# Memory keys and values, and the recurrence's values, in 512-column products instead of 256

## Chip, cores and metric

The kernel runs on one core of a Trainium2 chip. The metric is the device time of one execution in microseconds (us), the median of several runs. A smaller number is better. The profile is a trace of one execution on the same kind of chip.

## The reference, cut to what matters

Two layers of a decoder trunk on 512 tokens of width 1024, with 256 memory tokens, all in float32:

```python
mem_n = rmsnorm(mem, mem_norm)
for l in range(DEPTH):                                   # DEPTH = 2
    h = rmsnorm(x, norm_mix)
    (..., g_q, g_f, g_i, g_g, m_q, gate_logits) = split_cols(h @ w_in)
    y_a = a_b * causal_conv3(a_c * a_x, conv_w)          # branch A
    y_b = dsa_attention(q, k, d_v, iq, ik, iw)           # branch B: top-128 of the keys
    hv = g_i.reshape(b, s, HG_HEADS, HG_DV)              # the recurrence's values
    o_c = hgrn2_chunkwise(hq, hk, hv, log_f)             # branch C
    mk, mv = jnp.split(mem_n @ mem_w_kv, 2, axis=-1)     # 512 columns of keys, 512 of values
    mk = rmsnorm(mk.reshape(b, MEM_TOKENS, MEM_HEADS, MEM_HEAD_DIM), mem_k_norm)
    ...                                                  # branch M: cross-attention to mk, mv
    merged = sum(gates[n] * (branches[n] @ w_lift[n]) for n in range(4))
    x = x + merged @ w_out
    x = x + ffn(rmsnorm(x, norm_ffn))
```

## The kernel before, in words

Every large product runs as three matmuls. A float32 operand is split into a high part in the matmul's reduced format and a low rest, and `mm3` (lines 269 to 272) adds high by high, high by low and low by high into one accumulator tile. One matmul has a stationary tile of 128x128 and a moving operand of 256 or 512 columns.

Weights come through `Chunk` (line 211). One transfer on the SP queue brings 1024 KB (for instance 1024 rows by 256 columns, or 512 rows by 512 columns) into `w_raw`, which has 2 buffers. Two conversions follow, each for half of the chunk: ScalarE (ACT) writes `w_hi` and VectorE (DVE) writes `w_lo` (line 225). These pairs have 3 buffers (`W_BUFS`), and they are written with `high_priority`.

The accumulators are tiles of 128x512 float32 in three groups: `mm` with 3 buffers, `at` with 2, `tr` with 3. Products use `mm`. Attention scores, the index scores and the recurrence use `at`. Transposes and small sums use `tr`.

The order of the instructions on each engine is not the order in the source. The kernel is built with `schedule_with_timeline_sim=True`: a planner walks a simulated time line and gives each engine the ready instruction of the lowest number, where a number is the place in the source, lowered by 3000 in `high_priority`. An accumulator buffer goes to the first planned instruction that asks for it. The result is a fixed list for each engine.

The stages that the change touches:

1. **Start.** `mem_in_T` transposes the normalised memory into `mt`. `mem_kv(l)` (line 427) then makes keys and values of layer l, first for layer 0, woven with `first_h` (which makes `h` from `x`), and after `rope_tables` for layer 1. It goes over four column blocks of 256, two of keys and two of values. For each block it takes one chunk (all 1024 rows) and for each of the two token tiles 24 matmuls of 256 columns (`tokens`, line 250). For keys it copies the result to `ku`, sums squares per head, computes one norm for two heads by two token tiles, scales, transposes, and writes `kv` as a high and a low part. A transfer of 512 KB per block stores them in `kv_dram`.
2. **Mixer, the part around the attention of branch B.** In each layer `lift(3, y_m)` runs woven with `sel`, the selection of the 128 largest index scores (lines 824 and 825 on DVE). Then `weave(chain(lift(0, y_a), values(hv)), attend(0..3), R2)` writes one step of the first chain and three steps of attention in turn. `lift(n)` has four steps of 48 matmuls for two gate tiles and 24 for two tiles of `y`, all of 512 columns. `values(hv)` (line 667) has two steps, each with one chunk of 256 columns and four token tiles of 24 matmuls of 256 columns. `attend(t)` has two steps of four heads: scores into `at` (lines 685 and 686), a biased minimum on DVE (line 698), exponentials and scaling on ACT into `prob`, transposes (line 709) copied to `pt`, and products with `vt` (line 715) that end in `y_b`.
3. **Recurrence** (`hgrn`). `logits` makes `zf`, `zq`, `zg` (line 880 takes them out of `mm`). Its pool reuses the memory of the attention's tiles. `head` uses `hv`.

Of the kernel before, what the change touches and what calls it, by code (L numbers as in the profile page):

```python
# [12 lines left out]
F32 = mybir.dt.float32  # L13
# [56 lines left out]
def hybrid_trunk(ctx: ExitStack, tc: tile.TileContext, x, mem, positions, norm_mix, w_in, conv_w,  # L70
# [19 lines left out]
    def A(dst, src, func, **kw):  # L90
        name = tables.get(func)
        if name is not None and name != table["set"]:
            load = act.preload_act_table_set(name)
            for u in table["users"]:
                tc.add_manual_dep(load.ins, u.name, order, reason="table set")
            table.update(set=name, load=load.ins, users=[])
        i = act.activation(dst, src, func, **kw)  # L97
        if name is not None:
            tc.add_manual_dep(i.ins, table["load"].name, order, reason="table set")
            table["users"].append(i.ins)  # L100
        return i

    def mm_ps():
        return pmm.tile([P, 512], F32, name="mm")
# [4 lines left out]
    def tr_ps():  # L109
        return pat.tile([P, 512], F32, name="tr", bufs=TR_BUFS)  # L110

    def f(ap):
        return ap.bitcast(F32)
# [62 lines left out]
    def col(i):  # L176
        return prm[:, i:i + 1]
# [21 lines left out]
    def rstd_into(dst, ms, scratch, n):  # L199
        rstd(dst, ms, scratch(n), scratch(n))  # L200

    def small(n, name="small", bufs=12):
        return consts.tile([P, 8], F32, name=name, bufs=bufs)[:, :n]
# [32 lines left out]
    def wchunk(src, kt, n):  # L236
        return Chunk(src, kt, n)

    def pair(a, k, s=slice(None)):
        return a[0][:, k, s], a[1][:, k, s]  # L240
# [11 lines left out]
    def tokens(w, a, t, ps, k0=0, kt=None):  # L252
        kt = w.kt if kt is None else kt
        for k in range(k0, k0 + w.kt):
            mm3(ps, pair(a, k, slice(t * P, (t + 1) * P)), w.at(k - k0), k == 0, k == kt - 1)
# [11 lines left out]
    def mm3(ps, a, b, first, last):  # L267
        ah, al = a
        bh, bl = b
        pe.matmul(ps, ah, bh, start=first, stop=False)  # L270
        pe.matmul(ps, ah, bl, start=False, stop=False)  # L271
        pe.matmul(ps, al, bh, start=False, stop=last)  # L272
# [104 lines left out]
    mem_r = small(2, name="mem_r", bufs=1)  # L377
    mem_sq = sp.tile([P, D], F32, name="mem_sq")
    mt = (sp.tile([P, KD, MEM], F32R, name="mt_hi"), sp.tile([P, KD, MEM], F32R, name="mt_lo"))
    mem_r2, mem_r4 = small(4, name="mem_r2", bufs=1), small(4, name="mem_r4", bufs=1)  # L380

    def mem_in_T():
        for c in range(KD):
            ps = tr_ps()
            for t in range(2):
                pe.transpose(ps[:, t * P:(t + 1) * P], mem_in[:, t, c * P:(c + 1) * P], ident)
            A(mt[0][:, c, :], ps[:, :MEM], AF.Copy, scale=g_mem(c))
            dve.scalar_tensor_tensor(mt[1][:, c, :], ps[:, :MEM], g_mem(c), f(mt[0][:, c, :]),
                                     op0=OP.mult, op1=OP.subtract)
        for t in range(2):  # L390
            A(mem_sq, mem_in[:, t, :], AF.Square, scale=D ** -0.5, accum_out=mem_ss[:, t:t + 1])
        rstd_into(mem_r, mem_ss, small, 2)
        dve.tensor_copy(mem_r4.rearrange("p (a b) -> p a b", b=2), mem_r[:, :, None].to_broadcast([P, 2, 2]))
        dve.tensor_mul(mem_r2, mem_r4, mem_r4)

    norms = []
# [29 lines left out]

    def mem_kv(l):
        kv = sp.tile([P, 4, 2, 2, MEM], F32R, name="kv", bufs=1)
        for q in range(2):
            w = wchunk(mem_w_kv[l][:, q * 256:(q + 1) * 256], KD, 256)  # L430
            kus = []
            ms, r = small(4), small(4, "mk_r", 2)
            for t in range(2):
                ps = mm_ps()[:, :256]
                tokens(w, mt, t, ps)
                ku = sp.tile([P, 2, P], F32, name="ku", bufs=3)
                with tc.high_priority(offset=AHEAD):
                    A(ku.rearrange("p a b -> p (a b)"), ps, AF.Copy)
                for j in range(2):
                    sq = sp.tile([P, P], F32, name="mk_sq", bufs=2)  # L440
                    A(sq, ku[:, j, :], AF.Square, scale=P ** -0.5, accum_out=ms[:, 2 * t + j:2 * t + j + 1])
                kus.append(ku)
            dve.tensor_mul(ms, ms, mem_r2)
            rstd_into(r, ms, small, 4)
            dve.tensor_mul(r, r, mem_r4)
            for t in range(2):
                for j in range(2):
                    dve.tensor_scalar(kus[t][:, j, :], kus[t][:, j, :], r[:, 2 * t + j:2 * t + j + 1], None, op0=OP.mult)
            for j in range(2):
                ps = tr_ps()[:, :MEM]  # L450
                for t in range(2):
                    pe.transpose(ps[:, t * P:(t + 1) * P], kus[t][:, j, :], ident)
                hi, lo = kv[:, 2 * q + j, 0, 0, :], kv[:, 2 * q + j, 0, 1, :]
                A(hi, ps, AF.Copy, scale=col(76 + l))
                dve.scalar_tensor_tensor(lo, ps, col(76 + l), f(hi), op0=OP.mult, op1=OP.subtract)
            nc.scalar.dma_start(kv_dram[l][:, 2 * q:2 * q + 2, 0], f(kv[:, 2 * q:2 * q + 2, 0]))
            yield
        for q in range(2):
            w = wchunk(mem_w_kv[l][:, 512 + q * 256:512 + (q + 1) * 256], KD, 256)
            for t in range(2):  # L460
                ps = mm_ps()[:, :256]
                tokens(w, mt, t, ps)
                ps = ps.rearrange("p (h d) -> p h d", d=P)
                hi, lo = (kv[:, 2 * q:2 * q + 2, 1, e, t * P:(t + 1) * P] for e in range(2))
                A(hi, ps, AF.Copy, scale=mem_r[:, t:t + 1])
                dve.scalar_tensor_tensor(lo, ps, mem_r[:, t:t + 1], f(hi), op0=OP.mult, op1=OP.subtract)
            nc.scalar.dma_start(kv_dram[l][:, 2 * q:2 * q + 2, 1], f(kv[:, 2 * q:2 * q + 2, 1]))
            yield
    mem_in_T()
    steps(mem_kv(0), first_h())  # L470
    rope_tables()
# [29 lines left out]
    def mixer(l, h, norms, cm, cf):  # L501
# [11 lines left out]
        def lift(n, y, merged, last=None):  # L513
            def gates(m):
                gw = wchunk(w_in[l][:, C_GATE + n * D + m * P:C_GATE + n * D + (m + 2) * P], KD, 256)
                gs = [gate_tile()[:, :S] for _ in range(2)]
                for g, ps in zip(gs, features(gw, h, (0, 1))):
                    with tc.high_priority(offset=AHEAD):
                        dve.tensor_mul(g, ps, r_b)
                    sigmoid(g, g, mix.tile([P, S], F32, name="gate_e", bufs=1))  # L520
                return gs

            look = LOOK[l][n] == "1"
            ahead = gates(0) if look else None
            for m in range(0, KD, 2):
                if look:
                    gs, ahead = ahead, gates(m + 2) if m + 2 < KD else None
                else:
                    gs = gates(m)
                lw = wchunk(w_lift[l, n][:, m * P:(m + 2) * P], 4, 256)  # L530
                pls = features(lw, y, (0, 1))
                for i in range(2):
                    g, pl = gs[i], pls[i]
                    with tc.high_priority(offset=AHEAD):
                        if n == 3:
                            dve.tensor_mul(merged[:, m + i, :], g, pl)
                        else:
                            dve.tensor_mul(g, g, pl)
                            dve.tensor_add(merged[:, m + i, :], merged[:, m + i, :], g)
                    if last is not None:  # L540
                        last(m + i)
                yield
# [19 lines left out]
        def weave(main, back, ratio):  # L562
            for _ in main:
                for _ in range(ratio):
                    next(back, None)
            for _ in back:
                pass
# [97 lines left out]
                        yield  # L665

        def values(hv):
            for q in range(2):
                w = wchunk(w_in[l][:, C_GI + q * 256:C_GI + (q + 1) * 256], KD, 256)
                for t in range(NT):  # L670
                    ps = mm_ps()[:, :256]
                    tokens(w, h, t, ps)
                    A(hv[:, t, q * 256:(q + 1) * 256], ps, AF.Copy, scale=r_t[:, t:t + 1])
                yield

        with pool_("dsa") as dp:
            qS = dp.tile([P, 8, S], F32R, name="qS")
# [170 lines left out]
            hvs = cm.enter_context(ExitStack())  # L848
            hv = hvs.enter_context(pool_("hv", "left")).tile([P, NT, 512], F32, name="hv")
            with pool_("att", "left") as dp2:  # L850
                weave(chain(lift(0, y_a, merged), values(hv)), chain(*(attend(t, dp2, y_b) for t in range(NT))), R2)

        with pool_("hgrn") as hp:
            y_c = new_y()
# [261 lines left out]
```

## Time and profile before

| | |
|---|---|
| median of 3 runs | 2047.9 us (2047.63 to 2047.9) |
| profiled execution, its time | 2047.48 us |
| profiled execution, its span | 2045.4 us |
| PE (TensorE matmul) busy | 2034.5 us |
| DVE busy, ACT busy | 1269.3 us, 1017.5 us |
| matmuls | 10348 |

A row of a time line or of the chain reads: start in us, duration in us, engine, source line, operation, output tile <- input tiles, shape, count; in brackets the idle time just before it and what ended it. "PEld" is the load of a stationary tile, which overlaps "PE". The ends of matmuls are modelled, so that a matmul shown with 0.39 us can have its successor 0.23 us after its start. The distance between starts is therefore the pace of PE, and its busy time is not. Rows of a "windows" view give, for a stretch of the span, the busy time and the count of each engine, the granted TensorE clock ("PEclk") and the share of the transfer engines in use.

### The profile page before, as it was taken

Reading aid. Unit: us, or ns where it says so; the run is one execution under the profiler, and the core shown is the slowest. Engines: PE = TensorE matmul, PEld = TensorE weight load, DVE = VectorE, ACT = ScalarE, POOL = GpSimd, SP = SyncE. Lnnn points to the kernel's source line nnn. Section 1 sums busy time; section 2 is a strip of 40 time slices with the busy share of each in tenths; the row PEclk is TensorE's granted clock in tenths of the full one; section 3 lists DMA queues with packets and bytes.
Section 4 is the critical chain, followed back from the end, with each engine's and each line's share of the span. In section 5 each row is a group of like instructions: output and inputs, shape, how many; then the busy total and the mean of one; then the engine's idle time right before and its main releaser. Section 6 shows DMA issues by size and latency. Waiting matters only on the chain.

```text
span 2045.4 us, 26581 instructions
## 1 busy us (share of the span) xinstructions
PE 2034.5 (99%) x10348; PEld 1715.8 (84%) x10348; DVE 1269.3 (62%) x2507; ACT 1017.5 (50%) x1834; POOL 9.8 (0%) x33
## 2 busy tenths in 40 slices
PE   8999999999999999999999999999999999999999
PEld 8998988888888888888889898888888888888887
DVE  6779998547676544334457889963777754533442
ACT  7653655766665423223355456576767633322331
POOL 0000000000000000000000000000000000000000
PEclk9999999999999999999999999999999999999999
DMA  7632232223233232233243213322223322323322
GB/s 253 220 89 94 68 93 93 64 71 93 78 118 113 83 103 93 93 105 102 87 155 94 88 58 107 97 76 63 83 83 101 126 90 96 103 75 111 97 79 93
DMA packets 187709, 203.79 MB, mean 100 GB/s; under 512 B 4270, under 2 KB 176384, under 8 KB 187456
## 3 DMA queue, kind: packets, MB, share of 16 engines
q1 hardware_dynamic: 183872, 193.56, 29.8%
q10 hardware_dynamic: 3552, 8.41, 1.1%
q8 instruction: 81, 1.33, 0.3%
q14 instruction: 44, 0.36, 0.1%
q0 software_dynamic: 160, 0.13, 0.0%
HBM read 191.60 MB, written 10.49 MB: 99 GB/s over the span
## 4 chain that ended last, share of the span: by engine, by line
PE 99%; DMA 1%; DVE 0%; ACT 0%; SPq 0%; issue 0%; DVEq 0%
PE mm L270 30%; PE mm L272 30%; PE mm L271 30%; PE tr L715 1%; PE tr L709 1%; PE at L686 1%; PE at L685 1%; PE at L272 1%; PE at L270 1%; PE at L271 1%; DMA w_raw<-in_mem_w_kv_dram 1%; PE at L963 0%; PE at L937 0%; PE tr L653 0%; PE tr L754 0%; PE tr L972 0%
## 5 line engine op out<-in xcount | busy, mean ns | idle before, releaser
L270 PE MATMUL mm<-h_hi,w_hi 128*128 128x512 f32 x1664 | 653.0, 393 | 0.0
L271 PE MATMUL mm<-h_lo,w_hi 128*128 128x512 f32 x1664 | 652.1, 392 | 0.0
L272 PE MATMUL mm<-h_hi,w_lo 128*128 128x512 f32 x1664 | 650.1, 392 | 0.0
L225 DVE TENSOR_TENSOR w_lo<-w_raw,w_hi 128x1024 fp32r<-128x1024 f32 (+1 forms) x346 | 419.5, 1213 | 364.5 <-ACT w_hi L97 361.3
L97 ACT ACTIVATE w_hi<-w_raw 128x1024 fp32r<-128x1024 f32 (+1 forms) x346 | 363.4, 1051 | 460.8 <-PE mm L271 414.5
L272 PEld LDWEIGHTS mm<-h_hi,w_lo 128*128 128x128 f32 x1664 | 312.8, 188 | 64.8 <-issue 1.2
L270 PEld LDWEIGHTS mm<-h_hi,w_hi 128*128 128x128 f32 x1664 | 312.8, 188 | 64.5 <-issue 2.2
L271 PEld LDWEIGHTS mm<-h_lo,w_hi 128*128 128x128 f32 x1664 | 312.9, 188 | 63.8 <-issue 2.0
L272 PE MATMUL mm<-w_hi,h_lo 128*128 128x256 f32 (+1 forms) x448 | 128.2, 286 | 0.0
L271 PE MATMUL mm<-w_lo,h_hi 128*128 128x256 f32 (+1 forms) x448 | 127.0, 285 | 0.0
L270 PE MATMUL mm<-w_hi,h_hi 128*128 128x256 f32 (+1 forms) x448 | 127.0, 285 | 0.0
L271 PE MATMUL mm<-a_lo,w_hi 128*128 128x512 f32 x272 | 106.3, 391 | 0.0
L270 PE MATMUL mm<-a_hi,w_hi 128*128 128x512 f32 x272 | 106.0, 390 | 0.0
L272 PE MATMUL mm<-a_hi,w_lo 128*128 128x512 f32 x272 | 105.8, 391 | 0.0
L270 PE MATMUL mm<-y_hi,w_hi 128*128 128x512 f32 x256 | 101.4, 397 | 0.0
L272 PE MATMUL mm<-y_hi,w_lo 128*128 128x512 f32 x256 | 100.6, 393 | 0.0
L271 PE MATMUL mm<-y_lo,w_hi 128*128 128x512 f32 x256 | 100.3, 392 | 0.0
L272 PEld LDWEIGHTS mm<-w_hi,h_lo 128*128 128x128 f32 x448 | 85.8, 191 | 1.4 <-issue 0.8
L270 PEld LDWEIGHTS mm<-w_hi,h_hi 128*128 128x128 f32 x448 | 85.3, 191 | 1.2 <-issue 0.8
L271 PEld LDWEIGHTS mm<-w_lo,h_hi 128*128 128x128 f32 x448 | 85.6, 191 | 0.6
L97 ACT ACTIVATE a_hi<-fg 128x512 fp32r<-128x512 f32 x44 | 27.8, 633 | 109.4 <-DVE fg L1065 109.4
L97 ACT ACTIVATE prob<-prob,small 128x128 f32<-128x128 f32 (+3 forms) x128 | 69.2, 554 | 15.2 <-DVE small L698 14.6
(358 smaller groups left out, 2946.9 us busy)
## 6 DMA issues: line engine op xcount, KB each, us to landing
w_raw<-in_w_in_dram SPq DMA_DIRECT2D x72, 1024.0 KB, 5.3
w_raw<-in_ffn_w_up_dram SPq DMA_DIRECT2D x44, 1024.0 KB, 5.1
w_raw<-in_w_lift_dram SPq DMA_DIRECT2D x32, 512.0 KB, 3.5
w_raw<-in_ffn_w_down_dram SPq DMA_DIRECT2D x16, 1024.0 KB, 5.5
w_raw<-in_mem_w_kv_dram SPq DMA_DIRECT2D x8, 1024.0 KB, 5.4
w_raw<-in_w_out_dram SPq DMA_DIRECT2D x8, 1024.0 KB, 5.2
w_raw<-in_ffn_w_down_dram SPq DMA_DIRECT2D x10, 512.0 KB, 3.4
kv<-kv ACTq DMA_DIRECT2D x8, 512.0 KB, 3.2
```

The source lines that it names most:

```text
L97: i = act.activation(dst, src, func, **kw)
L225: dve.tensor_sub(lo, raw[:, k:e], f(hi))
L270: pe.matmul(ps, ah, bh, start=first, stop=False)
L271: pe.matmul(ps, ah, bl, start=False, stop=False)
L272: pe.matmul(ps, al, bh, start=False, stop=last)
L685: pe.matmul(ps, q[:, hh, s], k[0][:, :n], start=True, stop=False)
L686: pe.matmul(ps, q[:, hh, s], k[1][:, :n], start=False, stop=True)
L709: pe.transpose(pp[:, (2 * e + i) * P:(2 * e + i + 1) * P], probs[2 * i + e][:, b * P:(b + 1) * P], ident)
L715: pe.matmul(pv[e * HD:(e + 1) * HD, :], vt[:, b, :], pt[:, b, e * 2 * P:(e + 1) * 2 * P], start=b == 0, stop=b == t)
```

## The change

`mem_kv` makes all 512 columns of the keys in one pass and all 512 columns of the values in another. The weights come in halves of 512 rows by 512 columns, both token tiles keep their accumulator over the two halves, and each matmul has 512 columns. Norm, scaling and transposes are done once for four heads by two token tiles, and the two stores of a layer have 1024 KB each. `values` does the same for 512 columns: its two weight chunks are asked for together, and four accumulators collect at the same time, three `mm` and one `at`. In the chain it stands ahead of `lift(0)`, not behind it.

```diff
-    mem_r2, mem_r4 = small(4, name="mem_r2", bufs=1), small(4, name="mem_r4", bufs=1)
+    mem_r2, mem_r4 = small(8, name="mem_r2", bufs=1), small(8, name="mem_r4", bufs=1)
...
     def mem_kv(l):
         kv = sp.tile([P, 4, 2, 2, MEM], F32R, name="kv", bufs=1)
-        for q in range(2):
-            w = wchunk(mem_w_kv[l][:, q * 256:(q + 1) * 256], KD, 256)
...
-            for t in range(2):
-                ps = mm_ps()[:, :256]
-                tokens(w, mt, t, ps)
-                ku = sp.tile([P, 2, P], F32, name="ku", bufs=3)
...
+        def products(c0):
+            pss = [mm_ps() for _ in range(2)]
+            for k0 in (0, 4):
+                w = wchunk(mem_w_kv[l][k0 * P:(k0 + 4) * P, c0:c0 + 512], 4, 512)
+                for ks, _, _ in w.parts:
+                    for t, ps in enumerate(pss):
+                        for k in ks:
+                            mm3(ps, pair(mt, k0 + k, slice(t * P, (t + 1) * P)), w.at(k), k0 + k == 0, k0 + k == KD - 1)
+                if k0 == 0:
+                    yield None
+            yield pss
+
+        for pss in products(0):
+            if pss is None:
+                yield
+        ms, r = small(8), small(8, "mk_r", 2)
+        kus = []
+        for t, ps in enumerate(pss):
+            ku = sp.tile([P, 4, P], F32, name="ku", bufs=2)
+            with tc.high_priority(offset=AHEAD):
+                A(ku.rearrange("p a b -> p (a b)"), ps, AF.Copy)
...
+        nc.scalar.dma_start(kv_dram[l][:, :, 0], f(kv[:, :, 0]))
+        yield
+        for pss in products(512):
+            if pss is None:
+                yield
+        for t, ps in enumerate(pss):
+            ps = ps.rearrange("p (h d) -> p h d", d=P)
+            hi, lo = (kv[:, :, 1, e, t * P:(t + 1) * P] for e in range(2))
+            A(hi, ps, AF.Copy, scale=mem_r[:, t:t + 1])
+            dve.scalar_tensor_tensor(lo, ps, mem_r[:, t:t + 1], f(hi), op0=OP.mult, op1=OP.subtract)
+        nc.scalar.dma_start(kv_dram[l][:, :, 1], f(kv[:, :, 1]))
+        yield
...
         def values(hv):
-            for q in range(2):
-                w = wchunk(w_in[l][:, C_GI + q * 256:C_GI + (q + 1) * 256], KD, 256)
-                for t in range(NT):
-                    ps = mm_ps()[:, :256]
-                    tokens(w, h, t, ps)
-                    A(hv[:, t, q * 256:(q + 1) * 256], ps, AF.Copy, scale=r_t[:, t:t + 1])
-                yield
+            ws = [wchunk(w_in[l][k0 * P:(k0 + 4) * P, C_GI:C_GI + 512], 4, 512) for k0 in (0, 4)]
+            pss = [mm_ps() for _ in range(MM_BUFS)] + [at_ps()]
+            tokens_wide(ws, h, KD, pss)
+            for t, ps in enumerate(pss):
+                A(hv[:, t, :], ps, AF.Copy, scale=r_t[:, t:t + 1])
+            yield
...
-                weave(chain(lift(0, y_a, merged), values(hv)), chain(*(attend(t, dp2, y_b) for t in range(NT))), R2)
+                weave(chain(values(hv), lift(0, y_a, merged)), chain(*(attend(t, dp2, y_b) for t in range(NT))), R2)
```

More of the change, by code (lines that the diff above doesn't have):

```diff
@@ L392, in mem_in_T @@
         rstd_into(mem_r, mem_ss, small, 2)
-        dve.tensor_copy(mem_r4.rearrange("p (a b) -> p a b", b=2), mem_r[:, :, None].to_broadcast([P, 2, 2]))
+        dve.tensor_copy(mem_r4.rearrange("p (a b) -> p a b", b=4), mem_r[:, :, None].to_broadcast([P, 2, 4]))
         dve.tensor_mul(mem_r2, mem_r4, mem_r4)
@@ L428, in mem_kv @@
         kv = sp.tile([P, 4, 2, 2, MEM], F32R, name="kv", bufs=1)
-        for q in range(2):
-            w = wchunk(mem_w_kv[l][:, q * 256:(q + 1) * 256], KD, 256)
-            kus = []
-            ms, r = small(4), small(4, "mk_r", 2)
-            for t in range(2):
-                ps = mm_ps()[:, :256]
-                tokens(w, mt, t, ps)
-                ku = sp.tile([P, 2, P], F32, name="ku", bufs=3)
[L437 to L445, printed above, removed]
-            for t in range(2):
[L447 to L456, printed above, removed]
-            yield
@@ L458, in mem_kv @@
-        for q in range(2):
-            w = wchunk(mem_w_kv[l][:, 512 + q * 256:512 + (q + 1) * 256], KD, 256)
-            for t in range(2):
-                ps = mm_ps()[:, :256]
[L462 to L468, printed above, removed]
+        def products(c0):
[9 more added lines that the diff above has]
+            yield pss
@@ new lines, in mem_kv @@
+        for pss in products(0):
[7 more added lines that the diff above has]
+                A(ku.rearrange("p a b -> p (a b)"), ps, AF.Copy)
+            for j in range(4):
+                sq = sp.tile([P, P], F32, name="mk_sq", bufs=2)
+                A(sq, ku[:, j, :], AF.Square, scale=P ** -0.5, accum_out=ms[:, 4 * t + j:4 * t + j + 1])
+            kus.append(ku)
@@ new lines, in mem_kv @@
+        dve.tensor_mul(ms, ms, mem_r2)
+        rstd_into(r, ms, small, 8)
+        dve.tensor_mul(r, r, mem_r4)
+        for t in range(2):
+            for j in range(4):
+                dve.tensor_scalar(kus[t][:, j, :], kus[t][:, j, :], r[:, 4 * t + j:4 * t + j + 1], None, op0=OP.mult)
+        for j in range(4):
+            ps = tr_ps()[:, :MEM]
+            for t in range(2):
+                pe.transpose(ps[:, t * P:(t + 1) * P], kus[t][:, j, :], ident)
+            hi, lo = kv[:, j, 0, 0, :], kv[:, j, 0, 1, :]
+            A(hi, ps, AF.Copy, scale=col(76 + l))
+            dve.scalar_tensor_tensor(lo, ps, col(76 + l), f(hi), op0=OP.mult, op1=OP.subtract)
@@ L667, in values @@
         def values(hv):
-            for q in range(2):
-                w = wchunk(w_in[l][:, C_GI + q * 256:C_GI + (q + 1) * 256], KD, 256)
-                for t in range(NT):
-                    ps = mm_ps()[:, :256]
-                    tokens(w, h, t, ps)
-                    A(hv[:, t, q * 256:(q + 1) * 256], ps, AF.Copy, scale=r_t[:, t:t + 1])
-                yield
+            ws = [wchunk(w_in[l][k0 * P:(k0 + 4) * P, C_GI:C_GI + 512], 4, 512) for k0 in (0, 4)]
[4 more added lines that the diff above has]
+            yield
         with pool_("dsa") as dp:
```

## The prediction

> **What bounds the kernel.** I read the page first (busy times, then the chain that ended last), then the waits of PE, then PE's time line for the pace of its matmuls.
>
> ```profile
> PE 2034.5 (99%) x10348; PEld 1715.8 (84%) x10348; DVE 1269.3 (62%) x2507; ACT 1017.5 (50%) x1834; POOL 9.8 (0%) x33
> PE 99%; DMA 1%; DVE 0%; ACT 0%; SPq 0%; issue 0%; DVEq 0%
> ```
>
> The chain lies on PE for 99% of the span. The waits of PE, in full:
>
> ```profile
> PE tr L160 <- DMA rows<-in_mem_k_norm_dram: 1.9, 1, 1.9
> PE mm L271 <- DVE w_lo L225: 1.3, 2, 0.8
> PE tr L144 <- DVE ones_d L118: 1.1, 1, 1.1
> PE mm L270 <- ACT w_hi L97: 1.0, 1, 1.0
> PE tr L386 <- DVE mt_lo L388: 0.8, 2, 0.6
> ```
>
> All of them lie in the first 23 us. From there on PE goes from one matmul to the next, so a change is worth what it takes from the sum of PE's steps, less any new wait. Work saved on ACT, DVE or the queues is worth nothing by itself.
>
> **The pace.** Busy time misleads here, as ends are modelled. I take distances between starts, from stretches where nothing else runs.
>
> ```profile
> 53.90 0.28 PE L272 MATMUL mm<-w_hi,mt_lo 128*128 128x256 f32 x1
> ...
> 59.30 0.28 PE L272 MATMUL mm<-w_hi,mt_lo 128*128 128x256 f32 x1
> ```
>
> ```profile
> 319.86 0.39 PE L271 MATMUL mm<-h_lo,w_hi 128*128 128x512 f32 x1
> ...
> 326.88 0.39 PE L272 MATMUL mm<-y_hi,w_lo 128*128 128x512 f32 x1
> ```
>
> Between the first two rows lie 45 steps: 5.40 / 45 = 0.1200 us for 256 columns. Between the second two lie 31: 7.02 / 31 = 0.2265 us for 512. Two narrow matmuls replaced by a wide one save 2 x 0.1200 - 0.2265 = 0.0135 us. Each matmul thus carries about 13 ns that don't depend on its columns, and the change sheds one such piece per pair.
>
> **How many pairs.**
>
> ```profile
> L271 PE MATMUL mm<-w_lo,mt_hi x128: 278/283/416, 14.0 to 68.6; 128*128 128x256 f32 x128
> L97 ACT ACTIVATE hv<-mm,rstd_t x16: 453/466/481, 390.5 to 1414.0; 128x256 f32<-128x256 f32 x16
> ```
>
> Memory: 128 on each of three lines, 384 narrow matmuls, 192 pairs. Values: 16 evictions, each after 24 narrow matmuls (8 row blocks by three), again 384, 192 pairs. Together 384 pairs x 0.0135 = 5.2 us off PE.
>
> [...]
>
> **What of it is hidden.** The first chunk of memory weights gains nothing: PE then waits for the second.
>
> ```profile
> 7.79 12.02 DMA w_raw<-in_mem_w_kv_dram
> 19.84 1.07 ACT w_hi L97
> 20.93 1.24 DVE w_lo L225
> 22.21 0.39 PE L271 MATMUL mm<-w_lo,mt_hi 128*128 128x256 f32 x1 [0.56 <-DVE w_lo L225]
> ```
>
> Transfer, high part, low part, matmul: the chain steps off PE just here. The new second chunk has the same 1024 KB and the same two conversions, so PE would only wait 24 x 0.0135 = 0.3 us longer. Sum: -5.2 + 0.3 = -4.9 us. The bounds for this start are 2.1 us worse (if the chunk lands as late as the 7.8 us that one transfer took, against 5.7 in the middle) and 0.9 us better (the waits on `w_lo` and `w_hi` partly gone).
>
> ```profile
> 12.70:22.20 9.50, 8.11 (x51) 7.70 (x51) 6.35 (x18) 9.31 (x19) 0.00 (x0) 0.82 1.03 355
> 22.20:68.80 46.60, 46.49 (x388) 46.14 (x389) 36.64 (x109) 36.12 (x91) 0.52 (x1) 1.00 0.75 256
> DMA to landing us min/median/max: 5.1/5.7/7.8
> ```
>
> **Edits that I cost at nothing.** One norm for four heads makes fewer and longer steps on ACT and DVE; they run beside the value products, 48 x 0.2265 = 10.9 us of PE, and in the second row above DVE and ACT have 10 us of 46.6 free. Only the eight transposes per layer are PE's, as before. If that cover were gone, the chain of norms (some ten short ACT and DVE steps of 0.2 to 0.5 us, four scalings, about 5 us) would show once per layer. The stores, now of 1024 KB, and the release of the start pool have slack: layer 1's last transfer to `kv_dram` is issued at 80.8 us before and made ACT wait 2.6 us, but not PE. Evictions of 512 columns instead of two of 256 take less ACT time. The two chunks of `values` now stand ahead of `lift(0)`'s on the SP queue; one part feeds 24 matmuls, 5.4 us, and its two conversions take 2.3, so the third part buffer suffices. The same helper with three `mm` and one `at` accumulators already runs at the kernel's end without a wait of PE. No gain or loss for these; bounds -0.5 and +1.
>
> **The step that is moved.** The last accumulator of `values` and the place ahead of `lift(0)` meet the attention. In the seam:
>
> ```profile
> 307.93 0.22 PE L685 MATMUL at<-k_hi,qS 128*128 128x128 f32 x1
> ...
> 327.11 0.22 PE L686 MATMUL at<-k_lo,qS 128*128 128x128 f32 x1
> 327.17 0.28 PE L685 MATMUL at<-k_hi,qS 128*128 128x128 f32 x1
> ```
>
> ```profile
> 340.94 0.42 DVE L828 TENSOR_SCALAR bias<-score 128x512 f32<-128x512 f32 x1
> 341.28 0.68 DVE L209 SCALAR_TENSOR_TENSOR gate_e<-gate,gate_e 128x512 f32<-128x512 f32 x1
> 341.88 0.28 DVE L698 CUSTOM_DVE_ANT_0 prob<-at,causal_bias 128x128 f32<-128x128 f32 x1
> ```
>
> The first two heads' scores took both `at` buffers at 307.9 and 327.2, and DVE, busy with the selection, read the first at 341.9. `values` would start at 327.4 and need one of the two. Either it gets one (then attention has one buffer until `values` ends, 327.4 + 96 x 0.2265 = 349.1), or it waits for 342.2. And at the other end:
>
> ```profile
> 327.10:343.80 16.70, 16.70 (x77) 13.88 (x76) 15.99 (x34) 8.73 (x15) 0.00 (x0) 1.00 0.30 94
> 343.80:390.00 46.20, 46.20 (x245) 37.28 (x244) 29.12 (x81) 37.67 (x89) 0.00 (x0) 1.00 0.30 94
> 390.00:427.80 37.80, 37.80 (x285) 31.74 (x284) 13.97 (x45) 27.86 (x62) 0.00 (x0) 1.00 0.09 29
> 427.80:446.60 18.80, 18.80 (x97) 14.43 (x96) 5.84 (x8) 7.02 (x12) 1.49 (x4) 1.00 0.36 113
> 446.54 0.69 DVE L880 TENSOR_TENSOR zf<-mm,rstd 128x512 f32<-128x512 f32 x1 [3.75 <-PE tr L715]
> ...
> 1431.04 0.69 DVE L880 TENSOR_TENSOR zf<-mm,rstd 128x512 f32<-128x512 f32 x1 [3.75 <-PE tr L715]
> ```
>
> And from the groups of PE between 427.8 and 446.5:
>
> ```profile
> L271 PE MATMUL mm<-h_lo,w_hi 128*128 128x512 f32 x22 | 8.8, 402 | 0.0
> L270 PE MATMUL mm<-h_hi,w_hi 128*128 128x512 f32 x22 | 8.8, 401 | 0.0
> L272 PE MATMUL mm<-h_hi,w_lo 128*128 128x512 f32 x21 | 8.3, 395 | 0.0
> ```
>
> Attention needs PE's other work as cover: `lift(0)` to 390, the old `values` to 427.8, then the `logits` of the recurrence. The second `zf` can't leave its accumulator before the attention's last product (446.5), but PE isn't held yet: three `mm` buffers, one of them freed, carry 96 of these matmuls, and 22 + 22 + 21 = 65 had run. The slack is 31 x 0.2265 = 7.0 us. The new order replaces 192 x 0.12 = 23.0 us of cover behind the first step by one lift step of 16.7 (the first row): 6.3 us of the 7.0 are used up, 0.7 remain. Layer 1 shows the same pattern 984.5 us later (1431.04). I take nothing for it, as the attention has slack of its own: ACT is busy 65.5 of the 84 us from 343.8 to 427.8.
>
> **Forecast.** 2047.5 - 4.9 = 2042.6 us for the profiled execution; the median stands 0.4 above it: 2043.0. Own range 2041.5 to 2045.
>
> **Rivals.**
>
> *`values` waits for its borrowed accumulator.* For it: the rows at 307.9 and 327.2; what is ready takes the buffer. With three accumulators and three part buffers PE can do 3 x 18 = 54 matmuls, to 339.6, and then waits for 342.2: 2.6 us per layer, 5.2 for both, 2048.2. Against it: `values` puts no gate work on DVE in this stretch, so the selection ends up to 2 us earlier, and `values` has the lower number in the plan.
>
> *The attention comes too late, and PE stands before the recurrence.* The point from which it decides is 0.7 us of delay. For it: the busiest part of the attention loses its lightest companion. From 390 to 427.8 ACT gives `values` 6.4 us:
>
> ```profile
> L97 ACT ACTIVATE hv<-mm,rstd_t 128x256 f32<-128x256 f32 x7 | 3.3, 468 | 4.5 <-PE mm L272 4.5
> L97 ACT ACTIVATE w_hi<-w_raw 128x1024 fp32r<-128x1024 f32 x3 | 3.1, 1049 | 0.5 <-PE mm L272 0.5
> ```
>
> A lift step, in ACT's groups from 327.1 to 343.8:
>
> ```profile
> L97 ACT ACTIVATE w_hi<-w_raw 128x1024 fp32r<-128x1024 f32 x3 | 3.2, 1064 | 3.5 <-PE mm L271 3.5
> L97 ACT ACTIVATE gate<-gate_e 128x512 f32<-128x512 f32 x2 | 1.3, 632 | 3.7 <-DVE gate_e L209 3.7
> ```
>
> Three conversions and, for two gate tiles, four steps of some 0.62 us: 3.2 + 8 x 0.62 = 8.1 us per 16.7 of PE, thus 18.3 in 37.8: 27.9 - 6.4 + 18.3 = 39.8, 2 us more than there are; with attention one buffer short and one head later (2.4 us) the delay is 4.4, beyond the slack 3.7 per layer, 7.4 for both: 2050.4. Twice that delay (8.8, beyond the slack 8.1 per layer, 16.2 for both) gives 2059.2. Between them, 2053: slower. Against it: the work of ACT over the whole stretch is the same, and the first 22 us leave ACT and DVE freer than before. A wait of this length may also cost clock: in the first row of 12.70:22.20 the granted clock is 0.82, after the pauses of the start. [...]
>
> [...]
>
> **Chances.** Forecast 0.50, waiting accumulator 0.20, late attention 0.25, small fixed part and the rest 0.05. This kernel's runs can tell 0.2% from no change, 4.1 us: below 2043.8 is faster, above 2052.0 slower. Of the forecast four fifths lie below 2043.8, and a little of the rest (start better than thought): faster 0.43. The rest of the forecast, the first rival and two fifths of the second: same 0.34. Slower 0.23. The range takes in both rivals up to 2054, and 2041.3 below.
>
> **What would show it.** Right: 9964 matmuls, PE's pace 0.2265 in 22 to 66 us, `first_h`'s successor reached some 2.3 us earlier, the mixers' stretch from the seam to the recurrence shorter by 1.3 us in each layer, no new PE wait. Wrong: a wait of PE on DVE L698 (accumulator) near 340 and 1324 us, or on DVE L880 near 450 and 1434; a clock below 1.00 there; or a pace for 512 columns above 0.2265 when attention is mixed in.

## The result: four microseconds slower, and where they went

Measured: 2051.95 us, the median of 12 runs (2051.39 to 2056.25), against 2047.87 us for the kernel before (12 runs, 2047.49 to 2048.39). The ratio is 1.0024, with a 95% interval of 1.0016 to 1.0032; here and in the tables below it is taken over all runs, not from the two medians (which give 1.0020). The change makes the kernel slower by 4.1 us. The forecast was 2043.0 us. The profiled execution of the changed kernel took 2052.94 us, 1.0 above its median.

The page after, its first lines:

```profile
span 2050.8 us, 25759 instructions
PE 2034.3 (99%) x9964; PEld 1698.0 (83%) x9964; DVE 1271.7 (62%) x2495; ACT 1015.5 (50%) x1812; POOL 9.8 (0%) x33
```

The 384 matmuls are gone, 10348 - 9964, yet the span is 5.4 us longer (the spans are those of two executions; the medians differ by 4.1). The waits of PE after, cut to those that matter here (what PE waited for: us in total, times, longest):

```profile
PE mm L270 <- ACT hv L97: 3.4, 2, 1.7
PE mm L270 <- ACT w_hi L97: 2.4, 2, 2.0
PE tr L631 <- ACT sq L97: 2.0, 1, 2.0
...
PE tr L719 <- ACT pt L97: 0.9, 2, 0.5
```

Before, every wait lay in the first 23 us. Now there are new ones: on `sq`, on `hv`, on `pt`, and a longer one on `w_hi`.

To place the loss I follow matmuls that both kernels have. Their starts, from the time lines of PE, before and after:

| matmul | before | after | later by |
|---|---|---|---|
| first product of the first `h` stage (L270) | 68.84 | 68.93 | 0.09 |
| last index score of layer 0 (`at<-ik_hi`) | 296.32 | 302.22 | 5.90 |
| the same in layer 1 | 1280.82 | 1286.87 | 6.05 |
| last matmul of the kernel | 2040.53 | 2046.65 | 6.12 |

(What follows the last matmul is 0.7 us shorter after, so the spans differ by 5.4.) From 118 us of the kernel before to the second row the starts of PE stand 5.90 us apart throughout, and behind it almost nothing is added: the whole mixer with the new `values` costs 0.15 us in layer 0 and 0.07 in layer 1. The loss is made in the first 120 us, by the memory, although 192 of the pairs saved, 2.6 us, lie there. Three places carry it.

**The start.** PE's time line after, around the second chunk:

```profile
20.20 0.40 PE L272 MATMUL mm<-w_hi,mt_lo 128*128 128x512 f32 x1
20.44 0.38 PE L386 MATMUL tr<-ident,mem_in 128*128 128x128 f32 x2
22.85 0.91 PE L270 MATMUL mm<-w_hi,mt_hi 128*128 128x512 f32 x2 [2.02 <-ACT w_hi L97]
```

And ACT's:

```profile
20.86 0.47 ACT L97 ACTIVATE mt_hi<-tr,prm 128x256 fp32r<-128x256 f32 x1 [1.18 <-PE tr L386]
...
21.75 1.99 ACT L97 ACTIVATE w_hi<-w_raw 128x1024 fp32r<-128x1024 f32 x2
```

The second chunk's conversion begins at 21.75, where it began at 19.84 before. ACT stands idle for 1.18 us, waiting for the last pair of memory transposes. It isn't the transfer: in this execution that was asked for 0.7 us later than before (8.45 us, not 7.79), but in `mem_only` below it was asked for at 7.89, and ACT waited 1.67 us for the same transposes and began at 21.76. A wide first chunk holds only the first half of the rows and doesn't need them, so they stand behind its matmuls in PE's list (20.44). In ACT's rows the conversion (21.75) comes behind their eviction (20.86). PE waits 2.0 us. Then its clock drops to 0.56 (columns: stretch, length, busy time and count of PE, PEld, DVE, ACT, POOL, granted clock, share of the transfer engines, GB/s):

```profile
24.00:27.00 3.00, 2.90 (x8) 2.33 (x9) 2.93 (x7) 0.78 (x1) 0.00 (x0) 0.56 0.26 23
27.00:30.00 3.00, 3.00 (x15) 2.48 (x14) 1.27 (x4) 1.60 (x2) 0.00 (x0) 1.00 0.86 332
```

Eight matmuls fall into the first stretch, fifteen into the next one of the same length, at full clock. From the start to the first `h` product the kernel gains 2.6 us in pairs and ends 0.09 later: the start costs 2.7 us. (It is some 0.4 more if one counts that four key transposes of layer 1, which before stood ahead of the first `h` product, at 65.9 to 66.6 us, now stand behind it.)

**The key chain of layer 1.** PE before, where the last two key transposes are followed by the sums of `sq` without a wait:

```profile
79.08 0.38 PE L452 MATMUL tr<-ident,ku 128*128 128x128 f32 x2
...
83.09 0.95 PE L620 MATMUL tr<-ones_h,sq 128*128 128x1 f32 x8
```

PE after:

```profile
77.55 0.49 PE L464 MATMUL tr<-ident,ku 128*128 128x128 f32 x3
...
78.12 0.49 PE L464 MATMUL tr<-ident,ku 128*128 128x128 f32 x3
...
82.56 0.38 PE L464 MATMUL tr<-ident,ku 128*128 128x128 f32 x2
...
83.49 0.28 PE L272 MATMUL mm<-w_hi,h_lo 128*128 128x256 f32 x1
85.80 1.05 PE L631 MATMUL tr<-ones_h,sq 128*128 128x1 f32 x8 [2.03 <-ACT sq L97]
```

ACT after:

```profile
82.98 0.47 ACT L97 ACTIVATE kv<-tr,prm 128x256 fp32r<-128x256 f32 x1 [1.42 <-PE tr L464]
84.00 0.52 ACTq L468 DMA_DIRECT2D kv<-kv  x1
84.57 0.69 ACT L97 ACTIVATE qg_hi<-mm,prm 128x512 fp32r<-128x512 f32 x1 [1.12 <-DVE rope L370]
85.15 0.59 ACT L97 ACTIVATE sq<-mm 128x512 f32<-128x512 f32 x1
```

Six of the eight transposes go at 77.6 to 78.5, the last two 5 us after the first. They are the fourth head's. One norm for four heads asks for four `tr` tiles at once, and there are three. Behind those two stand, on ACT, the eviction, then the store of the keys, which waits for DVE's low part, and then the squares of the memory queries (`sq`). PE waits 2.03 us for them (from 83.49 to 85.80, less the matmul's own 0.12, it is 2.19). (The bracket at `qg_hi` names a step of the rope tables; the low part of these keys ended on DVE at 83.96, the store began at 84.00, and 0.52 of the 1.12 us are the issue of the store.)

**The clock behind that wait.**

```profile
82.00:86.00 4.00, 1.97 (x17) 1.77 (x16) 3.14 (x15) 1.91 (x4) 0.00 (x0) 1.00 1.07 381
86.00:90.00 4.00, 4.00 (x29) 4.00 (x28) 1.35 (x3) 1.34 (x5) 0.20 (x1) 0.76 0.62 237
90.00:94.00 4.00, 4.00 (x20) 4.00 (x20) 1.72 (x10) 2.81 (x11) 0.47 (x3) 0.50 0.00 0
94.00:98.00 4.00, 4.00 (x32) 4.00 (x31) 3.06 (x21) 2.70 (x13) 0.00 (x0) 0.89 0.00 0
```

After PE resumes at 85.80 the clock is still 1.00 from 86 to 88 us, and then 0.50 to 0.54 until 94.9. Lost, by an estimate from the three clocks below 1 in these rows: 4 x 0.24 + 4 x 0.50 + 4 x 0.11 = 3.4 us. With the 2.2 of the wait and the 0.4 of the four transposes that moved here it is 6.0, for 5.8 us that are added between the first two rows of the table. This is the account of one execution. In `mem_only` (below) PE has the same wait of 2.0 us and a clock of 1.00 behind it, and yet this stretch adds 4.1 us (from 69.22 to 300.82): PE comes earlier to the next chain and waits there too,

```profile
PE tr L664 <- DVE mprob L662: 1.2, 1, 1.2
```

a wait that the changed kernel doesn't have. So of the 3.4 us only some 1.7 (5.8 less 4.1) are the net price of the slow clock.

**The end of `values`.** PE and ACT after, layer 0:

```profile
313.83 0.39 PE L270 MATMUL at<-w_hi,h_hi 128*128 128x512 f32 x1
...
337.18 0.39 PE L272 MATMUL mm<-w_hi,h_lo 128*128 128x512 f32 x1
...
338.32 0.39 PE L272 MATMUL at<-w_hi,h_lo 128*128 128x512 f32 x1
340.43 0.50 PE L270 MATMUL mm<-h_hi,w_hi 128*128 128x512 f32 x1 [1.72 <-ACT hv L97]
```

```profile
338.74 1.06 ACT L97 ACTIVATE w_hi<-w_raw 128x1024 fp32r<-128x1024 f32 x1 [4.55 <-PE at L272]
339.71 1.83 ACT L97 ACTIVATE hv<-mm,rstd_t 128x512 f32<-128x512 f32 x3
```

All three `mm` accumulators belong to `values` to its end; the last product into one of them starts at 337.18, and the next stage needs one of them. ACT, idle for 4.55 us, has first a weight conversion in its list that waits for the last of the value matmuls, and only then the evictions. PE stands from 338.55 to 340.43, 1.9 us, and again in layer 1. That eats what the 96 pairs of each layer save (1.3 us) and the little that the stretch behind gains.

### The profile page after: what moved, and what is told of

Read it like the earlier page. It is cut to its first block, busy times and chain, and to the rows that moved or that the text cites. A ratio compares the mean times of both kernels' runs of the same rounds, so it can differ in the third digit from the quotient of the medians.

```text
span 2050.8 us, 25759 instructions
## 1 busy us (share of the span) xinstructions
PE 2034.3 (99%) x9964; PEld 1698.0 (83%) x9964; DVE 1271.7 (62%) x2495; ACT 1015.5 (50%) x1812; POOL 9.8 (0%) x33
## 4 chain that ended last, share of the span: by engine, by line
PE 99%; DMA 1%; ACT 0%; DVE 0%; issue 0%; DVEq 0%; SPq 0%; ACTq 0%
PE mm L270 30%; PE mm L271 30%; PE mm L272 30%; PE tr L725 1%; PE tr L719 1%; PE at L696 1%; PE at L695 1%; PE at L272 1%; PE at L270 1%; PE at L271 1%; PE tr L631 0%; PE at L973 0%; PE at L947 0%; PE tr L664 0%; PE tr L764 0%; PE tr L982 0%
## 5 line engine op out<-in xcount | busy, mean ns | idle before, releaser
L270 PE MATMUL mm<-h_hi,w_hi 128*128 128x512 f32 x1664 | 653.6, 393 | 3.4 <-ACT hv L97 3.4
L270 PEld LDWEIGHTS mm<-h_hi,w_hi 128*128 128x128 f32 x1664 | 312.7, 188 | 68.9 <-ACT hv L97 4.3
L272 PE MATMUL mm<-w_hi,h_lo 128*128 128x256 f32 (+2 forms) x368 | 110.9, 302 | 0.0
L271 PE MATMUL mm<-w_lo,h_hi 128*128 128x256 f32 (+2 forms) x368 | 110.2, 300 | 0.0
L270 PE MATMUL mm<-w_hi,h_hi 128*128 128x256 f32 (+2 forms) x368 | 109.6, 301 | 0.0
L270 PE MATMUL mm<-a_hi,w_hi 128*128 128x512 f32 x272 | 105.9, 389 | 0.0
L270 PE MATMUL mm<-y_hi,w_hi 128*128 128x512 f32 x256 | 100.8, 395 | 0.0
L97 ACT ACTIVATE prob<-prob,small 128x256 f32<-128x256 f32 (+3 forms) x128 | 69.6, 555 | 21.9 <-DVE small L708 19.2
L271 PEld LDWEIGHTS mm<-w_lo,h_hi 128*128 128x128 f32 x368 | 71.3, 194 | 2.1
L272 PEld LDWEIGHTS mm<-w_hi,h_lo 128*128 128x128 f32 x368 | 71.2, 194 | 1.9
L270 PEld LDWEIGHTS mm<-w_hi,h_hi 128*128 128x128 f32 x368 | 71.0, 194 | 1.9
```

## The experiments

In the tables and texts below each time stands against the kernel before on the same chip.

### The two parts, and the two halves of the values part

`mem_only` has the new `mem_kv` and the old `values` and chain; `val_only` the opposite. `move_only` only swaps the chain, `width_only` only has the new `values`:

```diff
# move_only
-weave(chain(lift(0, y_a, merged), values(hv)), chain(*(attend(t, dp2, y_b) for t in range(NT))), R2)
+weave(chain(values(hv), lift(0, y_a, merged)), chain(*(attend(t, dp2, y_b) for t in range(NT))), R2)
```

> The memory part alone; values as before. Theory: the traces put nearly all of the loss here (192 pairs -2.6 us, the later second chunk and its slow clock +2.7, the wait of PE on the squares of the memory queries near 83.6 us with the slow clock behind it +5.6), so 2047.9 + 5.7 or, with a shorter slow phase, about 2051.5 us, with the PE wait near 83.6 us in the profile. Rival, the prediction's own steps (pairs -2.6, start +0.3): 2045.6 us, the loss being the values'.

> The values part alone (512 columns, borrowed accumulator, ahead of the first lift); memory as before. Theory: 192 pairs -2.6 us against two waits of PE of some 2 us at the end of the values and a small gain elsewhere: 2048.1 us (2047.5 to 2048.8). Rival, late attention before the recurrence: 2050.4 or more, with PE waiting near 450 and 1434 us. Rival, no cost: 2045.3 us.

> Only the place: 256-column values ahead of the first lift, memory as before. Theory (the wait at the end of the values comes from all accumulators ending together): no such wait, 2047.9 us within 0.8. Rival, the place itself makes the attention late: 2050 or more.

> Only the width: 512-column values with the borrowed accumulator, behind the first lift as before, memory as before. Theory: -2.6 us of pairs; at the end of the values the recurrence's logits must again wait for the evictions, but there fewer weight conversions stand before them on ACT: 2045.3 to 2047.5 us. Rival, the borrowed accumulator starves the attention, which is in its last third there: above 2049 us.

| kernel | us | before | difference | ratio, 95% interval |
|---|---|---|---|---|
| mem_only | 2052.22 | 2047.68 | +4.5 | 1.0024 (1.0015 to 1.0033) |
| val_only | 2047.93 | 2047.68 | +0.3 | 1.0001 (0.9993 to 1.0010) |
| move_only | 2071.53 | 2047.68 | +23.9 | 1.0116 (1.0102 to 1.0130) |
| width_only | 2051.52 | 2047.68 | +3.8 | 1.0019 (1.0010 to 1.0028) |

The first two settle it: the loss is the memory's, and the values part is worth nothing. My theory fell with the other two. I had the place alone at no cost; it costs 24 us. The waits of PE in `move_only`:

```profile
PE at L685 <- DVE small L698: 21.4, 2, 10.7
```

PE's list has the third attention score there after 72 of the 192 value matmuls; the 72nd starts at 319.73. The score needs an `at` buffer, and the first two scores leave theirs only when DVE, after the selection, takes its first minimum:

```profile
319.73 0.28 PE L272 MATMUL mm<-w_hi,h_lo 128*128 128x256 f32 x1
330.68 0.48 PE L685 MATMUL at<-k_hi,qS 128*128 128x128 f32 x1 [10.67 <-DVE small L698]
```

```profile
330.00 0.43 DVE L828 TENSOR_SCALAR bias<-score 128x512 f32<-128x512 f32 x1
330.34 0.28 DVE L698 CUSTOM_DVE_ANT_0 prob<-at,causal_bias 128x128 f32<-128x128 f32 x1
```

So PE stands 10.7 us per layer, with value matmuls queued behind a score that can't start. The width alone, in the old place, costs 3.8 us, or 6.4 with the 2.6 that its pairs save. PE has these new waits, both in the attention:

```profile
PE tr L708 <- ACT prob L97: 2.2, 2, 1.1
PE tr L708 <- ACT pt L97: 0.9, 2, 0.5
```

They are 3.1 us; the other 3.3 I couldn't assign. That the `at` buffer is missing to an attention that has no other cover there would explain the waits, but no run tests it. Each half alone is bad, and both together are even: the two parts of this change can't be priced one by one.

### Which of the two mends the other?

`val_tr` is `val_only` with the fourth accumulator from `tr`:

```diff
-pss = [mm_ps() for _ in range(MM_BUFS)] + [at_ps()]
+pss = [mm_ps() for _ in range(MM_BUFS)] + [tr_ps()]
```

> The values part alone as in val_only (2047.93 us), the fourth accumulator borrowed from tr, not from at, so that the attention keeps both at buffers. If the borrowed at buffer alone keeps the attention's third score behind the values (it stood ahead of them in move_only and cost 10.7 us per layer), this goes as badly as move_only, above 2060 us. If the width does it (values in one run of 96 matmuls), 2048 us within 0.8.

It took 2048.09 us (before 2047.55; 1.0003, 0.9994 to 1.0012). The borrowed `at` buffer is not what keeps the score in its place; the wide form is, with its one run of 96 matmuls into four accumulators. Why the planner lets a score in between narrow products and not between wide ones, I didn't settle.

### The evictions first

`val_hv` is `val_only` with the four evictions in `high_priority`:

```diff
+with tc.high_priority(offset=AHEAD):
     for t, ps in enumerate(pss):
         A(hv[:, t, :], ps, AF.Copy, scale=r_t[:, t:t + 1])
```

> The values part alone (as in val_only, 2047.93 us), with the four evictions of hv written at the priority of the weight conversions. Theory: PE waits some 2 us per layer at the end of the values because ACT has a weight conversion, which itself waits for the last value matmul, ahead of the evictions; with the evictions first the wait goes: 2043.9 us (2043.3 to 2045). Rival: the next stage's weights set the wait anyway, 2047 us or more.

2047.83 us (before 2047.49; 1.0001, 0.9992 to 1.0010). But this tells nothing of the cause, as ACT's order is the same:

```profile
333.13 1.06 ACT L97 ACTIVATE w_hi<-w_raw 128x1024 fp32r<-128x1024 f32 x1 [4.55 <-PE at L272]
334.09 1.83 ACT L97 ACTIVATE hv<-mm,rstd_t 128x512 f32<-128x512 f32 x3
```

### The start, and the store of the keys

`mt_mm` gives the last memory transpose a free `mm` accumulator; `k_store_pool` issues the store of the keys from POOL's queue; `combo` has both and the edit of `val_hv`:

```diff
# mt_mm, in mem_in_T
-ps = tr_ps()
+ps = tr_ps() if c < KD - 1 else mm_ps()
# k_store_pool
-nc.scalar.dma_start(kv_dram[l][:, :, 0], f(kv[:, :, 0]))
+nc.gpsimd.dma_start(kv_dram[l][:, :, 0], f(kv[:, :, 0]))
```

> The changed kernel (2051.95 us) with the last of the eight memory transposes written into a free mm accumulator, not a fourth tr tile. Theory: that transpose no longer stands behind the first chunk's matmuls, so ACT converts the second chunk some 1.5 to 1.9 us earlier, PE's wait near 22 us shrinks and the slow clock behind it with it: 2049.5 us (2048.5 to 2050.5). Rival, the transfer of the second chunk sets this time: 2051.9 us.

> The changed kernel (2051.95 us) with the store of the keys issued from POOL's queue. Theory: the store, waiting for DVE on ACT's queue at 84 us, holds the squares of the memory queries back by 1.1 us; PE's wait near 83.6 us falls from 2.0 to some 0.9 us: 2050.9 us, and 2047.6 if the slow clock behind the wait goes too. Rival, the late last transposes alone make the wait: 2051.9 us.

> The changed kernel with all three edits (hv first, the last memory transpose in mm, key store on POOL's queue). Theory, the sum: 2051.95 - 4 - 2.5 - (1.1 to 4.4) = 2041.1 to 2044.4 us, below the kernel before. Rival, the waits move on to the next one in the queue: above 2046 us.

| kernel | us | before | difference | ratio, 95% interval |
|---|---|---|---|---|
| mt_mm | 2054.62 | 2047.49 | +7.1 | 1.0033 (1.0020 to 1.0047) |
| k_store_pool | 2049.57 | 2047.49 | +2.1 | 1.0013 (1.0004 to 1.0023) |
| combo | 2052.81 | 2047.49 | +5.3 | 1.0024 (1.0015 to 1.0034) |

`k_store_pool` did as expected: the wait on `sq` fell from 2.0 to 0.8 us, no slow clock followed (mean clock of this execution 0.997, of the changed kernel's 0.996), and half of the changed kernel's loss went (+4.1 to +2.1). `mt_mm` missed by 5 us, on the wrong side. The wait on `w_hi` at 22 us is gone, and the first `h` product starts at 64.85 us, 4.1 earlier than in the changed kernel, but the waits of PE are now

```profile
PE tr L631 <- ACT sq L97: 4.0, 1, 4.0
...
PE tr L413 <- DVE diag L412: 1.8, 1, 1.8
PE tr L464 <- DVE ku L460: 1.4, 1, 1.4
```

PE comes earlier to the key chain of layer 1, whose end is set by ACT and DVE, and waits there for all that it had won (its last index score of layer 0 starts at 302.20, that of the changed kernel at 302.22), and the clock falls again (0.61 and 0.53 from 84 to 92 us). This was its fastest execution, 2052.97 us; the other four lie 1.5 to 2.5 us above it at a lower mean clock (0.996 to 0.997, against 0.998), and where they lost that isn't in a trace. `combo`, 8 us above the upper end of what I wrote, shows the next in line: the wait on `sq` is down to 0.8 us, and PE waits 2.3 us for the transfer `mk<-kv`, with half clock behind it (mean clock of this execution 0.996). Its third edit did nothing, as in `val_hv`: the wait on `hv` is still 3.4.

### The fourth head's buffer

`k_at` takes a free `at` accumulator for the fourth head; `k_at_mt` adds the edit of `mt_mm`; `k_at_mt_rope` also writes layer 1's memory stage ahead of the rope tables:

```diff
# k_at, in mem_kv
-ps = tr_ps()[:, :MEM]
+ps = (tr_ps() if j < 3 else at_ps())[:, :MEM]
# k_at_mt_rope, besides
-    rope_tables()
     steps(mem_kv(1))
+    rope_tables()
```

> The changed kernel (2051.95 us) with the transposes of the fourth key head written into a free at accumulator, not a fourth tr tile. Theory: four heads at once need four tr tiles and there are three; the fourth pair of transposes stands 5 us behind the others (82.56 against 77.55 us), the store and the squares of the memory queries behind it on ACT. With a fourth buffer the wait near 83.6 us and its slow clock go: 2051.95 - 5.5 = 2046.5 us (2045.5 to 2047.5). Rival, DVE's other work (rope tables) makes the chain late: wait unchanged or only shorter, 2049 us or more.

> k_at together with mt_mm (last memory transpose in a free mm accumulator). Theory: mt_mm won some 3.5 us at the start and lost it in the key chain of layer 1; with the fourth buffer only the wait for the scaled keys near 73 us (1.5 us) remains: 2046.5 - 2 = 2044.5 us (2043.5 to 2046). Rival, the chain's end is fixed by ACT and DVE whenever PE comes: 2047 us or more.

> k_at_mt with layer 1's memory stage written ahead of the rope tables. Theory: the key chain's short DVE steps no longer stand between the rope tables' steps, the wait near 73 us goes as well: 2043 us (2042 to 2044.5). Rival, the rope tables come late for the queries behind, PE waits there: 2046 us or more.

| kernel | us | before | difference | ratio, 95% interval |
|---|---|---|---|---|
| k_at | 2049.00 | 2047.55 | +1.5 | 1.0006 (0.9997 to 1.0015) |
| k_at_mt | 2045.04 | 2047.55 | -2.5 | 0.9988 (0.9979 to 0.9997) |
| k_at_mt_rope | 2054.41 | 2047.55 | +6.9 | 1.0032 (1.0020 to 1.0045) |

With a fourth buffer the wait on `sq` isn't in the list any more, in `k_at` and `k_at_mt`. `k_at` stayed 2.5 us short of what I had written. Its start still has the 2.0 us wait, and in its profiled execution (1.2 us above its median) the half clock behind it lasts longer than in that of the changed kernel (there 0.67 and 1.00 in the two stretches below), so that the first `h` product comes at 70.31 us, not 68.93:

```profile
24.00:28.00 4.00, 4.00 (x10) 3.13 (x11) 2.84 (x8) 0.44 (x1) 0.00 (x0) 0.50 0.45 131
28.00:32.00 4.00, 4.00 (x14) 3.15 (x14) 1.23 (x1) 2.19 (x6) 0.00 (x0) 0.75 0.42 141
```

With both mended, in `k_at_mt`, the first `h` product comes at 65.05 us, 3.8 earlier than before the change (the pairs' 2.6, the 0.4 of the moved transposes and some of the old start's wait), later waits take some back, and 2.5 us remain, with the values part still even. The last kernel missed: the rope tables now come late for the queries, and PE waits for `qg_lo` (3.7 us) and `mk<-kv` (2.8), with half clock from 84 to 96 us (mean clock of this execution 0.995).

### One `mm` buffer left free

`val_2mm` is `val_only`, `best_2mm` is `k_at_mt`, both with other accumulators; `best_2tr` takes two of `tr` and none of `at`:

```diff
-pss = [mm_ps() for _ in range(MM_BUFS)] + [at_ps()]
+pss = [mm_ps(), mm_ps(), tr_ps(), at_ps()]          # val_2mm, best_2mm
+pss = [mm_ps(), mm_ps(), tr_ps(), tr_ps()]          # best_2tr
```

> The values part alone as in val_only (2047.93 us), with the four accumulators taken from two mm, one tr and one at buffer, so that one mm buffer stays free for the next stage. Theory: in val_only and in the changed kernel the third mm buffer comes late (the lift before it still holds it) and all three are held at the end, so that PE waits some 2 us per layer for an eviction that stands behind a weight conversion on ACT; with one mm buffer free PE goes on with 12 matmuls of the next stage and the wait goes: 2047.93 - 4 = 2043.9 us (2043.3 to 2045), the 192 pairs and a little more. Rival, the next stage's weights set the wait: 2047 us or more.

> k_at_mt (2045.04 us) with the same four accumulators (two mm, one tr, one at) for the values. Theory, sum of both: 2045.04 - 4 = 2041.0 us (2040.4 to 2042.2), which is the prediction's 384 pairs and some of the start. Rival, weights: above 2044 us.

> As best_2mm with two tr buffers in place of tr and at, so that the attention has both at buffers but one tr buffer until the values are out. Theory: same end of the values, 2041 us; if the borrowed at buffer delays the attention's first scores and with them the recurrence, this one is the faster by some 0.5 us; if the one tr buffer left does, the slower.

| kernel | us | before | difference | ratio, 95% interval |
|---|---|---|---|---|
| val_2mm | 2045.13 | 2047.59 | -2.5 | 0.9988 (0.9979 to 0.9997) |
| best_2mm | 2042.29 | 2047.59 | -5.3 | 0.9973 (0.9962 to 0.9984) |
| best_2tr | 2039.94 | 2047.59 | -7.7 | 0.9961 (0.9949 to 0.9974) |

The wait on `hv` is in none of them; it was the `mm` buffers, not the next weights. The time of `val_2mm` is 1.2 us above what I wrote, and its gain about that of its 192 pairs (2.6). `best_2mm`, both parts mended, saves 5.3 us where the prediction had 4.9 for all. That the two are so near is chance in part: against the kernel before, its trace has 2.4 us in the two mixers, where the pairs of the values are worth 2.6, but 2.1 up to the last index score of layer 0, with new and old waits in it, and 0.7 behind the last matmul, where no pair was merged. `best_2tr` is the fastest, and beats both kernels. All waits of PE over 0.4 us in it:

```profile
PE tr L160 <- DMA rows<-in_mem_k_norm_dram: 1.6, 1, 1.6
PE tr L144 <- DVE ones_d L118: 1.1, 1, 1.1
PE tr L386 <- DVE mt_lo L388: 1.1, 2, 0.6
PE mm L270 <- DVE qg_lo L628: 0.7, 1, 0.7
PE at L270 <- DMA mk<-kv: 0.5, 1, 0.5
```

Against `best_2mm` the wait for `pt` (0.9 us) is gone, as the attention has both `at` buffers. The other 1.5 us of the 2.4 between them I could not assign. By the traces, 1.1 us arise in each layer's mixer (from the last index score of layer 0 to that of layer 1: 983.3 and 982.3 us, before 984.5); the wait for `pt` is 0.45 of each. So `best_2tr` gains more than its pairs there, and why is open.

## Why the prediction was wrong, step by step

- **The bound and the pace: right.** PE stays at 99%, and the saving per pair holds: in the changed kernel 65 steps of 512 columns lie between 316.78 and 331.51 us, 0.2266 each, and the mended values give 2.5 us for 192 pairs, against 2.6 worked out from the two paces. The chances also give 0.05 to a small fixed part and the rest. No run shows a fixed part below 13 ns: the 2.5 us over 192 pairs are 13 ns a pair again. The 5.3 us of `best_2mm` for all 384 pairs don't add to this, as they hold more than pairs.
- **"What of it is hidden" (0.3 us, bound 2.1 worse): wrong.** It cost 2.7. I took the chain transfer, conversion, conversion, matmul from the trace of before and asked only whether the transfer would be later. I didn't ask what stands ahead of the conversion on ACT: the eviction of transposes which the new first chunk no longer needs, and which PE therefore did later. With a buffer of another pool for the last of them (`mt_mm`, `k_at_mt`) this wait is gone and the first `h` product is some 4 us earlier. And I priced the wait without the clock.
- **"Edits that I cost at nothing": the step that failed most.** I named the cover of the four-head norm, and the store at 80.8 us that made ACT wait, and took both as slack. I counted matmuls and ACT steps of the batch, but not its `tr` tiles, four where there are three. In its place the trace shows 2.2 us of wait and 3.4 of slow clock (1.7 net); `k_at` and `k_at_mt` show the wait gone with the fourth buffer, and `k_at` took back 2.6 of the 4.1 us. The sum's bound for these edits was +1.
- **The waiting accumulator, the first rival: right place and size, other mechanism.** 2.6 us per layer near 340 and 1324 were written, some 2 near 338 and 1323 came. That the size fits is luck. PE didn't wait to borrow `at`: I had let the values begin at 327.4 us, but the fourth tile had its `at` buffer from 313.8 us on. The stage behind waited to get an `mm` buffer back. I had taken the kernel's end, where the helper runs without a wait, as evidence; but there nothing follows that needs an accumulator.
- **The late attention, the second rival: didn't come.** No wait on `zf` shows. But the move and the width alone, at +24 and +4 us, show that it was near, by other ways than I had priced: a score put too early in PE's list and, not shown, one `at` buffer less.
- **The signs.** For slower I gave 0.23, and the only case named for it was the attention, whose share by the text is three fifths of 0.25, 0.15; likewise "same" adds up to 0.37 at least and not 0.34. Of the signs of being right, only the count of matmuls and the pace came: the first `h` product was reached 0.09 us later and not 2.3 earlier, and the mixers were not shorter by 1.3 each. The mechanism that decided, a buffer count in a stage that I had called covered, had no place among the cases.

## What to carry to other kernels

PE, busy 99% of the time here, saved 13 ns for each pair of matmuls made one, but the price is asked of the buffers: count the tiles that the larger batch holds at one time, of every pool, and what queues in order behind the one that has to wait. Leave the next stage one accumulator of the kind that it begins with. An edit that makes PE earlier is worth something only as far as the next chain that ACT and DVE end; mend that first, or the two together (`mt_mm` alone made the loss 7.1 us from 4.1; with `k_at` it turned +1.5 into -2.5).

## What the hardware showed that I had not expected

In these traces a pause of PE cost more than its length at some places and not at others. Each of the two waits of 2.0 us after was followed by half clock (0.56 from 24 to 27 us, 0.50 from 90 to 94). In `mem_only` the same wait on `sq` of 2.0 us, at the same place, has none:

```profile
82.00:86.00 4.00, 2.06 (x18) 1.86 (x16) 3.32 (x14) 1.61 (x4) 0.00 (x0) 1.00 1.06 368
86.00:90.00 4.00, 3.91 (x33) 3.91 (x34) 1.57 (x3) 1.30 (x4) 0.00 (x0) 1.00 0.77 299
90.00:94.00 4.00, 4.00 (x36) 4.00 (x35) 1.71 (x10) 2.52 (x10) 0.66 (x3) 1.00 0.00 0
```

The pauses on `hv` (1.7 us, in both layers of the changed kernel) have none either: the clock is 1.00 from 330 to 350 us and from 1315 to 1335. Behind longer pauses it came in these traces: 2.3 us in `combo` (mean clock 0.996), 4.0 in `mt_mm` (0.61 and 0.53 from 84 to 92 us), and 10.7 in `move_only`, where it fell within the pause and was still 0.50 from 330 to 334 us.

So the same wait of 2.0 us had two outcomes, and what decides between them these traces don't show. The runs are spread as well: the changed kernel's lie 4.9 us apart, those of before 0.9. The mean clock that was recorded with each run goes the same way: 0.995 in the two runs above 2056 us, 0.996 in the three at 2053, 0.997 in the seven below. That the spread is the clock's is thus likely; behind which pause it arises, no trace shows.
